# Two gate blocks computed with the first input projections, stick-breaking attention started earlier, and h written in pairs of k-tiles

## The chip, the cores and the metric

One core of a Trainium2 chip runs the whole layer. The metric is the device time of one execution in microseconds, the median of several runs. All data are float32 in memory; large matrix products are made of three products of split halves, as told below.

## What is computed

One decoder layer on 256 tokens of width 2048. The part around the change is the modulated norm, the one wide input projection and the third gate:

```python
mod = (jax.nn.silu(c) @ w_ada[l] + b_ada[l]).reshape(B, N_MOD, 1, D)
sh1, sc1, gt1, sh2, sc2, gt2 = (mod[:, j] for j in range(N_MOD))
h = rmsnorm(x, g_mix[l]) * (1.0 + sc1) + sh1
z = h @ w_in[l]
(mq, mk, mv, mo, mi, mf, dq, dk, dv, sq, sk, sv, gm, gd, gs) = split_cols(z, IN_SIZES)
...
merged = (jax.nn.sigmoid(gm) * (out_m @ w_branch[l, 0])
          + jax.nn.sigmoid(gd) * (out_d @ w_branch[l, 1])
          + jax.nn.sigmoid(gs) * (out_s @ w_branch[l, 2]))
x = x + gt1 * (merged @ w_out[l])
```

out_m, out_d and out_s are the three mixers (mLSTM, differential attention, stick-breaking attention). A gated MLP follows. w_in is 2048 x 16392, w_ada is 2048 x 12288.

## The kernel before

Every weight tile is loaded as float32 by the SP queue (`weights`, L344), rounded to a high part hi by ScalarE (L349), and its remainder lo is formed by VectorE (L351). A product is hi with both halves of the activation and lo with the high half: three matmuls for each k-tile of 128 rows and each 128 tokens (`gemm`, `mms`, L398; for blocks with features on the output partitions, L403, where the moving side is 256 tokens wide). A tick after each group of up to four k-tiles calls two queues of generators, `ada` and `side`, at the rates in `rates`: `ada` does the vector-matrix products with w_ada on VectorE (L230, L232), `side` the attention work. The order in which instructions then stand on each engine is set by a scheduler.

h needs the shift and scale, and these need w_ada: 33.6 MB for the 16 k-tiles of h. So the first projections are made in visits. `first` lists 13 column blocks (two each of sq, sk and sv of 512 columns, and seven of 440 that hold the small gates, dq, dk and dv). `visit(cis, kt1, rate)` takes the blocks `cis` on from the k-tile they had reached to k-tile kt1 (`partial`), while w_ada for the next k-tiles is loaded and multiplied in between. `make_h` (L465) writes h one k-tile at a time (ht L476 and hi L425 on ScalarE, lo L426 on VectorE), for k-tiles 0 and 1 first, 2 and 3 next (`ada_first(2)`), and then four at a time (`ada_quad`, whose VectorE products go into the tile quads). A partial sum goes to SBUF by a ScalarE copy (L556) and comes back into PSUM before the next visit by another (L545); the last visit adds it on VectorE (L558). Blocks 0 and 1 stay in PSUM (kept).

```python
visit(range(0, 9), 2, 0.62)
visit(range(9, 13), 4, 1.9)
visit(range(0, 9), 4, 1.0)
visit(range(0, 10), 8, 1.72)
visit(range(10, 13), 12, 1.36)
visit(range(0, 7), 12, 1.36)
```

After these visits h is whole. The 13 blocks are finished one after the other; when block 5 is done, stick-breaking attention (`stick`, 28 steps) joins the `side` queue. Then the first two blocks of the third gate are ordinary products over all 16 k-tiles with a sigmoid (`gates`, L860), `side` is drained, and differential attention (`diff`) joins while the other two gate blocks run. The rest (branches, mLSTM, output projection, MLP) isn't touched.

Weight loads of four k-tiles and w_ada loads share four buffers (three of rawp, and slot s3 for every fourth); loads of two k-tiles have three (tag ada). hi and lo have four buffers each, of two k-tiles.

Of the kernel before, what the change touches and what calls it, by code (L numbers as in the profile page):

```python
# [10 lines left out]
F32 = mybir.dt.float32  # L11
F32R = mybir.dt.float32r
AF = mybir.ActivationFunctionType
# [4 lines left out]
P = 128  # L18
S = 256
# [16 lines left out]
C_GM, C_GD, C_GS = 10248, 12296, 14344  # L36
# [3 lines left out]
def kernel(  # L40
# [14 lines left out]
    adap = ctx.enter_context(tc.tile_pool(name="adap", bufs=3))  # L55
# [7 lines left out]
    def slot(i, name):  # L63
        n = NT * MH * (MDH + 1) + 8 if i == 2 else 2048
        return slots.tile([P, n], F32, tag=f"s{i}", name=name)

    def bank(name):
        return mx.tile([P, 512], F32, tag="mx", name=name)

    def wide(name):  # L70
        return tmp.tile([P, 512], F32, tag="wide", name=name, bufs=3)

    def sidewide(name):
        return tmp.tile([P, 512], F32, tag="sidewide", name=name, bufs=4)

    def small(name):
        return tmp.tile([P, 256], F32, tag="small", name=name, bufs=3)

    V, A, T = nc.vector, nc.scalar, nc.tensor
# [111 lines left out]
    side = deque()  # L191
    ada = deque()
    state = {"ada": 0.0, "side": 0.0, "split": None, "load": None, "hold": None, "h": 0, "spare": None}

    def pump(queue, n):
        done = 0
        while queue and done < n:
            try:
                next(queue[0])
                done += 1  # L200
            except StopIteration:
                queue.popleft()

    def drain(queue):
        pump(queue, 1 << 30)

    rates = {"ada": 0.0, "side": 1.0}

    def tick():
        for key, queue in (("ada", ada), ("side", side)):  # L210
            state[key] += rates[key]
            n = int(state[key])
            state[key] -= n
            pump(queue, n)
# [65 lines left out]
    def ada_quad(k0, acc):  # L280

        for q in range(8):
            raw = raw_tile(2, 1024, "raw4")
            for i in range(2):
                r0, c0 = q * 256, i * D + k0 * P
                with tc.issue_after(state["load"].ins):
                    nc.sync.dma_start(raw[:, :, i * 512:(i + 1) * 512],
                                      w_ada[r0:r0 + 256, c0:c0 + 512].rearrange("(k p) f -> p k f", p=P))
            for k in range(2):
                ada_mac([acc], raw[:, k:k + 1, :], 2 * q + k, 1)  # L290
                yield
        ada_sums([acc], k0, 4)
# [39 lines left out]
    a1 = const.tile([P, KD], F32, name="a1")  # L332
    b1 = const.tile([P, KD], F32, name="b1")
# [89 lines left out]
    def split(hi, lo, src):  # L423

        A.copy(hi, src)  # L425
        return V.tensor_tensor(lo, src, hi.bitcast(F32), ALU.subtract)  # L426


    h1 = [slots.tile([P, KD // 2, 2 * S], F32R, tag=t, name="h1") for t in ("hh", "hl")]
# [3 lines left out]
    xnT_k = lambda kt: xnT[kt // 8][:, (kt % 8) * S:(kt % 8 + 1) * S]  # L433
# [29 lines left out]
            A.copy(xnT[k2 // 4][:, (k2 % 4) * 512:(k2 % 4 + 1) * 512], pb)  # L463

    def make_h(kt0, kt1):  # L465
        ts = []
        for kt in range(kt0, kt1):
            t = small("ht")
            ts.append(t)
            hi, lo = hact[0](kt), hact[1](kt)  # L470
            if kt0 == 0:
                A.activation(hi, xnT_k(kt), AF.Identity, scale=a1[:, kt:kt + 1], bias=b1[:, kt:kt + 1])
                V.tensor_scalar(t, xnT_k(kt), a1[:, kt:kt + 1], b1[:, kt:kt + 1], ALU.mult, ALU.add)
                state["split"] = V.tensor_tensor(lo, t, hi.bitcast(F32), ALU.subtract)
            else:
                A.activation(t, xnT_k(kt), AF.Identity, scale=a1[:, kt:kt + 1], bias=b1[:, kt:kt + 1])  # L476
                state["split"] = split(hi, lo, t)
        if kt0 == 0:
            state["first"] = state["split"]
        state["h"] = kt1  # L480
# [19 lines left out]
    def dest_D(i):  # L500
        def f(b):
            pieces = []
            for lo_, hi_, t in ((0, 8, None), (8, 1032, dq), (1032, 2056, dk), (2056, 3080, dv)):
                s_, e_ = max(lo_, i * 440), min(hi_, (i + 1) * 440)
                if s_ >= e_:
                    continue
                if t is None:
                    d = zif[:, b, s_:e_]
                else:
                    d = t[:, b * MW + s_ - lo_:b * MW + e_ - lo_]  # L510
                pieces.append((slice(s_ - i * 440, e_ - i * 440), d))
            return pieces
        return f

    first = []
# [5 lines left out]
        first.append(("T", C_SV + ch * 512, 512, dest_T(sv, ch), 1.0))  # L521
    for i in range(7):
        first.append(("T", C_IF + 440 * i, 440, dest_D(i), 1.0))

    def shaped(src, dst):
        return src.rearrange("p (a b) -> p a b", a=dst.shape[1]) if len(dst.shape) == 3 else src

    def partial(ci, kt0, kt1):
        orient, col0, n, dest, scale = first[ci]
        while state["h"] < kt1:  # L530
            pump(ada, 1)
        if kt0 == 0 and ci == 0:
            state["first"], done = state["mac0"], state["first"]
        pin = kt0 == 0 and ci < 2
        if kt0 == 0 and ci < 2:
            kept[ci] = [bank("kept"), bank("kept")]
        acc = kept.get(ci)


        put = acc is None and 0 < kt0 and kt1 < KD and not (kt1 == 4 and ci in (6, 8))  # L540
        if put:
            acc = [gp.tile([P, 512], F32, tag="gp", name="gp") for _ in range(2)]
            for b in range(2):
                for cs, d in dest(b):
                    A.copy(shaped(acc[b][:, cs], d), d)  # L545
        acc = gemm(orient, hact, w_in, 0, col0, n, kt0, kt1, hold=state["first"] if pin else None, hold_all=pin,
                   acc=acc)
        if kt0 == 0 and ci == 0:
            state["first"] = done
        for b in range(2):  # L550
            for cs, d in dest(b):
                if ci in kept:
                    if kt1 == KD:
                        A.activation(d, shaped(acc[b][:, cs], d), AF.Copy, scale=scale)
                elif put or kt0 == 0:
                    A.copy(d, shaped(acc[b][:, cs], d))  # L556
                else:
                    V.scalar_tensor_tensor(d, shaped(acc[b][:, cs], d), scale, d, ALU.mult, ALU.add)  # L558
        tick()

    kept = {}
# [1 line left out]
    quads = slot(4, "quads")  # L563
    ada.append(ada_first(2))
    ada.extend(ada_quad(k0, quads[:, (i % 2) * 1024:(i % 2 + 1) * 1024]) for i, k0 in enumerate((4, 8, 12)))
    done = [0] * 13

    def visit(cis, kt1, rate):
        rates["ada"] = rate
        for ci in cis:  # L570
            partial(ci, done[ci], kt1)
            done[ci] = kt1

    visit(range(0, 9), 2, 0.62)
    visit(range(9, 13), 4, 1.9)
    visit(range(0, 9), 4, 1.0)
    side.append(late_vectors())
    rates["side"] = 0.4
    visit(range(0, 10), 8, 1.72)
    visit(range(10, 13), 12, 1.36)  # L580
    visit(range(0, 7), 12, 1.36)
    drain(ada)
    drain(side)
    state["spare"] = None
# [270 lines left out]
    mg = []  # L855

    def gates(col_g, ch, dst):
        acc = gemm("T", hact, w_in, 0, col_g + ch * 512, 512, 0, KD)
        for tt in range(NT):
            A.activation(dst[tt], acc[tt], AF.Sigmoid)  # L860
        tick()

    def mg_of(ch):
        o = (ch % 2) * 512
        return [mg[ch // 2][:, tt * 1024 + o:tt * 1024 + o + 512] for tt in range(NT)]
# [31 lines left out]
        yield from ada_columns(4, bsc2_c, a2, gffn_c)  # L897

    ada.append(ada_rest())
    rates["side"] = 2.4  # L900
    for ci in range(13):
        partial(ci, done[ci], 16)
        if ci == 5:
            side.append(stick())


    rates["side"] = 2.0
    rates["ada"] = 0.9
    mg.append(slot(8, "mg0"))
    for ch in range(2):  # L910
        gates(C_GS, ch, mg_of(ch))
    drain(side)
    mg.append(slot(9, "mg1"))
    side.append(diff())
# [8 lines left out]
    for ch in range(2):  # L923
        acc = gemm("T", hact, w_in, 0, C_MO + ch * 512, 512, 0, KD)
# [6 lines left out]
    for ch in range(2):  # L931
        acc = gemm("T", hact, w_in, 0, C_MV + ch * 512, 512, 0, KD)
# [5 lines left out]
    for t, col0, f0 in ((mqT, C_MQ, 0), (mkT, C_MK, 8)):  # L938
        for ch in range(2):
            acc = gemm("H", h1act, w_in, 0, col0 + ch * 512, 512, 0, KD)  # L940
# [44 lines left out]
    for ch in range(4):  # L985
        acc = gemm("T", mact, w_out, 0, ch * 512, 512, 0, KD)
        cs = slice(ch * 512, (ch + 1) * 512)
        for tt in range(NT):
            t = wide("t512")
# [15 lines left out]
        for tt in range(NT):  # L1005
# [5 lines left out]
            with tc.issue_after(m.ins) if last else nullcontext():  # L1011
                for i in range(4):
                    k = 4 * ch + i
                    m = T.transpose(pbs[i // 2][:, (i % 2) * S + tt * P:(i % 2) * S + (tt + 1) * P],
                                    x2[tt][:, k * P:(k + 1) * P], ident)
        for i in range(4):
            k = 4 * ch + i
# [13 lines left out]
    k = 0  # L1031
    while k < KD:
# [4 lines left out]
        for j in range(m):  # L1037
            b = b2[:, k + j:k + j + 1]
            hi, lo = h2act(k + j)[:, 0:S], h2act(k + j)[:, S:2 * S]
# [9 lines left out]
    for half, (c0, c1) in enumerate(((0, 6), (6, NCH))):  # L1049
# [37 lines left out]
        for n in range(4):  # L1087
            acc = gemm("T", act, w_down, c0 * 512, n * 512, 512, 0, 4 * (c1 - c0))
            cs = slice(n * 512, (n + 1) * 512)
            for tt in range(NT):  # L1090
                t = wide("t512")
# [34 lines left out]
```

## Time and profile before

| | |
|---|---|
| median of 3 runs | 1785.43 us (1785.31 to 1785.56) |
| the profiled execution's own time | 1786.68 us |
| its span, first to last instruction | 1785.0 us |
| TensorE matmul busy | 1762.3 us (99%) |
| VectorE busy | 1302.2 us (73%) |
| ScalarE busy | 954.2 us (53%) |
| HBM traffic | 236 GB/s over the span |

The span is what the profiler saw between the first and the last instruction; the 1.7 us around it are in the execution's own time. Busy shares are averages over stages that differ, so the stretches are looked at one by one further down.

### The profile page before, as it was taken

Reading aid. Unit: us, or ns where it says so; the run is one execution under the profiler, and the core shown is the slowest. Engines: PE = TensorE matmul, PEld = TensorE weight load, DVE = VectorE, ACT = ScalarE, POOL = GpSimd, SP = SyncE. Lnnn points to the kernel's source line nnn. Section 1 sums busy time; section 2 is a strip of 40 time slices with the busy share of each in tenths; the row PEclk is TensorE's granted clock in tenths of the full one; section 3 lists DMA queues with packets and bytes.
Section 4 is the critical chain, followed back from the end, with each engine's and each line's share of the span. In section 5 each row is a group of like instructions: output and inputs, shape, how many; then the busy total and the mean of one; then the engine's idle time right before and its main releaser. Section 6 shows DMA issues by size and latency. Waiting matters only on the chain.

```text
span 1785.0 us, 23783 instructions
## 1 busy us (share of the span) xinstructions
PE 1762.3 (99%) x9168; PEld 1514.4 (85%) x9168; DVE 1302.2 (73%) x1734; ACT 954.2 (53%) x1338; POOL 16.7 (1%) x44
## 2 busy tenths in 40 slices
PE   7989999999999999999999999999999999999998
PEld 6889999888778888888888888888888888888887
DVE  6878656888878688777986577888875556666654
ACT  6667555676566566544444555555553345555432
POOL 2000000000000000000000000000000000000000
PEclk9999999999999999999999999999999999999999
DMA  9989755867767667688996557777765555555563
GB/s 330 361 315 336 281 175 166 281 223 250 252 232 260 212 219 252 230 281 285 323 307 212 185 165 247 258 258 268 267 202 201 191 189 189 189 189 189 189 214 116
DMA packets 219730, 423.33 MB, mean 237 GB/s; under 512 B 9026, under 2 KB 31674, under 8 KB 219104
## 3 DMA queue, kind: packets, MB, share of 16 engines
q1 hardware_dynamic: 217328, 417.44, 68.6%
q0 software_dynamic: 1008, 2.23, 0.4%
q10 hardware_dynamic: 1280, 2.14, 0.3%
q8 instruction: 72, 1.18, 0.3%
q14 instruction: 42, 0.34, 0.1%
HBM read 419.68 MB, written 2.10 MB: 236 GB/s over the span
## 4 chain that ended last, share of the span: by engine, by line
PE 96%; DMA 2%; DVE 1%; ACT 0%; issue 0%; SPq 0%; DVEq 0%
PE gp L398 55%; PE acch L384 32%; PE gp L403 2%; PE kept L403 2%; DMA raw<-in_w_ada_dram 1%; PE psc L688 1%; DMA raw<-in_w_in_dram 0%; PE pm L248 0%; DVE quads L232 0%; SPq L271 0%; PE pr L329 0%; DVE lo L351 0%; PE pa L713 0%; PE pm L238 0%; PE pmg L886 0%
## 5 line engine op out<-in xcount | busy, mean ns | idle before, releaser
L351 DVE TENSOR_TENSOR lo<-raw,hi 128x1024 fp32r<-128x1024 f32 (+1 forms) x608 | 724.8, 1208 | 363.0 <-ACT hi L349 325.9
L349 ACT CAST hi<-raw 128x1024 fp32r<-128x1024 f32 (+1 forms) x608 | 619.2, 1039 | 551.0 <-PE gp L398 348.7
L398 PE MATMUL gp<-hi,h 128*128 128x512 f32 (+1 forms) x1600 | 412.5, 386 | 2.1 <-ACT hi L349 1.0
L384 PE MATMUL acch<-h,hi 128*128 128x512 f32 x1664 | 403.6, 391 | 0.2 <-DVE h L1041 0.2
L384 PEld LDWEIGHTS acch<-h,hi 128*128 128x128 f32 x1664 | 303.4, 188 | 58.3 <-DVE h L1041 1.1
L398 PEld LDWEIGHTS gp<-hi,h 128*128 128x128 f32 x1600 | 295.8, 188 | 54.9 <-ACT hi L349 2.8
L398 PE MATMUL gp<-lo,h 128*128 128x512 f32 (+1 forms) x800 | 228.3, 383 | 0.0
L384 PEld LDWEIGHTS acch<-h,lo 128*128 128x128 f32 x1664 | 217.3, 191 | 10.8
L384 PE MATMUL acch<-h,lo 128*128 128x256 f32 x1664 | 220.8, 282 | 0.0
L232 DVE SCALAR_TENSOR_TENSOR acc<-araw,ccol,acc 128x512 f32<-128x512 f32 x240 | 179.0, 746 | 2.8 <-DMA araw<-in_w_ada_dram 1.1
L398 PEld LDWEIGHTS gp<-lo,h 128*128 128x128 f32 x800 | 149.7, 188 | 25.3 <-issue 0.3
L398 PE MATMUL gp<-hi,atl 128*128 128x512 f32 x352 | 137.0, 389 | 0.0
L398 PE MATMUL gp<-hi,ath 128*128 128x512 f32 x352 | 136.9, 389 | 0.0
L398 PE MATMUL gp<-lo,ath 128*128 128x512 f32 x352 | 105.8, 389 | 0.0
L398 PEld LDWEIGHTS gp<-lo,ath 128*128 128x128 f32 x352 | 66.1, 188 | 13.8
L398 PEld LDWEIGHTS gp<-hi,ath 128*128 128x128 f32 x352 | 66.1, 188 | 13.8
L398 PEld LDWEIGHTS gp<-hi,atl 128*128 128x128 f32 x352 | 66.0, 188 | 13.7
L232 DVE SCALAR_TENSOR_TENSOR quads<-raw,ccol,quads 128x1024 f32<-128x1024 f32 x45 | 57.7, 1281 | 11.1 <-DMA raw<-in_w_ada_dram 10.6
L398 PE MATMUL gp<-hi,mgl 128*128 128x512 f32 x128 | 50.3, 393 | 0.0
L398 PE MATMUL gp<-hi,mgh 128*128 128x512 f32 x128 | 50.0, 392 | 0.0
L1066 DVE SCALAR_TENSOR_TENSOR y<-gsum,cols,y 128x255 f32<-128x255 f32 (+1 forms) x88 | 41.4, 478 | 3.3 <-ACT y L1064 2.9
L403 PE MATMUL kept<-h,hi 128*128 128x256 f32 x256 | 39.1, 290 | 2.9 <-ACT h L425 1.1
(365 smaller groups left out, 1605.3 us busy)
## 6 DMA issues: line engine op xcount, KB each, us to landing
raw<-in_w_in_dram SPq DMA_DIRECT2D x98, 1024.0 KB, 5.1
raw<-in_w_up_dram SPq DMA_DIRECT2D x88, 1024.0 KB, 5.1
araw<-in_w_ada_dram SPq DMA_DIRECT2D x128, 512.0 KB, 5.9
raw<-in_w_down_dram SPq DMA_DIRECT2D x44, 1024.0 KB, 5.1
raw<-in_w_ada_dram SPq DMA_DIRECT2D x62, 512.0 KB, 7.4
raw<-in_w_branch_dram SPq DMA_DIRECT2D x24, 1024.0 KB, 6.3
raw<-in_w_in_dram SPq DMA_DIRECT2D x25, 880.0 KB, 5.6
raw<-in_w_out_dram SPq DMA_DIRECT2D x16, 1024.0 KB, 5.0
```

Of the source, the lines that this page charges most:

```text
L232: state["mac"] = V.scalar_tensor_tensor(acc, raw[:, k, :], ccol[:, kt:kt + 1], acc, ALU.mult, ALU.add)
L349: A.copy(hi[:, :, :n], raw[:, k0:k0 + 2, :n])
L351: state["split"] = V.tensor_tensor(lo[:, :, :n], raw[:, k0:k0 + 2, :n], hi[:, :, :n].bitcast(F32), ALU.subtract)
L384: T.matmul(acc[t][:, 0:m], lhsT=w[k // 2][:, k % 2, sl], rhs=ah(s0 + k)[:, 0:m], start=start, stop=s0 + k == kt1 - 1 and w is (wh if flip ...
L398: T.matmul(o, lhsT=a(s0 + k)[:, sl], rhs=wk[:, :n], **kw)
L403: T.matmul(o, lhsT=wk[:, sl], rhs=a(s0 + k), **kw)
L688: T.matmul(pcs[cc][:, o], lhsT=qT[cp, qs], rhs=kT[cp, ks], start=True, stop=True)
L1066: V.scalar_tensor_tensor(yf[:, sft:S], src[:, 0:S - sft], wc(2 - sft), yf[:, sft:S], ALU.mult, ALU.add)
```

## The change

Two column blocks of the third gate (columns C_GS to C_GS + 1024) become blocks 13 and 14 of `first`. Their partial sums lie in four tiles of 512 columns that are idle at that time: one accumulator tile of w_ada (tag acc) and three of the tag wide. Their last visit adds the sum on VectorE and applies the sigmoid from SBUF. The list of visits and its rates change. stick is appended at the same place, after block 5, but blocks 13, 6 to 12 and 14 with more k-tiles left now follow, at the side rate 2.6 instead of 2.4, and w_ada for the MLP starts at rate 0.5 there instead of after the 13 blocks. For k-tiles from 2 on, make_h rounds and splits two k-tiles with one instruction each.

```diff
     def make_h(kt0, kt1):
-        ts = []
-        for kt in range(kt0, kt1):
-            t = small("ht")
-            ts.append(t)
+        for kt in range(kt0, kt1, 1 if kt0 == 0 else 2):
             hi, lo = hact[0](kt), hact[1](kt)
...
             else:
-                A.activation(t, xnT_k(kt), AF.Identity, scale=a1[:, kt:kt + 1], bias=b1[:, kt:kt + 1])
-                state["split"] = split(hi, lo, t)
+                t = sidewide("ht")
+                for j in range(2):
+                    A.activation(t[:, j * S:(j + 1) * S], xnT_k(kt + j), AF.Identity, scale=a1[:, kt + j:kt + j + 1],
+                                 bias=b1[:, kt + j:kt + j + 1])
+                both = h1[kt // 8][:, kt % 8:kt % 8 + 2, :]
+                state["split"] = split(both[:, :, 0:S], both[:, :, S:2 * S], t.rearrange("p (k s) -> p k s", k=2))
...
+    gsp = []
+    for ch in range(2):
+        first.append(("T", C_GS + ch * 512, 512, lambda b, ch=ch: [(slice(0, 512), gsp[ch][b])], 1.0))
...
                     V.scalar_tensor_tensor(d, shaped(acc[b][:, cs], d), scale, d, ALU.mult, ALU.add)
+                    if ci > 12:
+                        A.activation(mg_of(ci - 13)[b], d, AF.Sigmoid)
...
     visit(range(0, 9), 2, 0.62)
-    visit(range(9, 13), 4, 1.9)
-    visit(range(0, 9), 4, 1.0)
+    gsp.extend([[adap.tile([P, 512], F32, tag="acc", name="gsp", bufs=2), wide("gsp")], [wide("gsp"), wide("gsp")]])
+    visit(range(9, 15), 4, 1.4)
+    visit(range(0, 9), 4, 1.15)
     side.append(late_vectors())
     rates["side"] = 0.4
-    visit(range(0, 10), 8, 1.72)
-    visit(range(10, 13), 12, 1.36)
-    visit(range(0, 7), 12, 1.36)
+    visit([13, 14, *range(0, 10)], 8, 1.55)
+    visit([*range(10, 13)], 8, 1.55)
+    visit([13, 14, *range(0, 6)], 12, 1.55)
...
-    rates["side"] = 2.4
-    for ci in range(13):
+    mg.append(slot(8, "mg0"))
+    for ci in (*range(6), 13, *range(6, 13)):
         partial(ci, done[ci], 16)
         if ci == 5:
             side.append(stick())
-
-
-    rates["side"] = 2.0
-    rates["ada"] = 0.9
-    mg.append(slot(8, "mg0"))
-    for ch in range(2):
-        gates(C_GS, ch, mg_of(ch))
+            rates["ada"], rates["side"] = 0.5, 2.6
+
+
+    rates["ada"], rates["side"] = 0.9, 2.0
+    partial(14, done[14], 16)
     drain(side)
```

Where instructions stand now, at three places. The first is VectorE at the start of the visits to k-tile 8: the remainders (lo) of w_in tiles and the products with w_ada (quads). In the kernel before:

```order
L351 TENSOR_TENSOR lo_1166<-raw_1159,hi_1165 128x1024
L232 SCALAR_TENSOR_TENSOR quads_308<-raw4_1218,ccol_124,quads_308 128x1024 x2
L232 SCALAR_TENSOR_TENSOR quads_308<-raw4_1287,ccol_124,quads_308 128x1024 x2
L351 TENSOR_TENSOR lo_1229<-raw_1226,hi_1228 128x1024
L351 TENSOR_TENSOR lo_1233<-raw_1226,hi_1232 128x1024
L351 TENSOR_TENSOR lo_1314<-raw_1311,hi_1313 128x1024
```

And in the changed kernel, where raw_1177 is the first four-k-tile load of block 13 and raw_1221 that of block 14:

```order
L426 TENSOR_TENSOR h1_138<-ht_1108,h1_138 128x2x256
L351 TENSOR_TENSOR lo_1151<-raw2_1148,hi_1150 128x2x440
L351 TENSOR_TENSOR lo_1180<-raw_1177,hi_1179 128x1024
L351 TENSOR_TENSOR lo_1184<-raw_1177,hi_1183 128x1024
L232 SCALAR_TENSOR_TENSOR quads_308<-raw4_1213,ccol_124,quads_308 128x1024
L563 SCALAR_TENSOR_TENSOR dq_304<-gp_1146,dq_304 128x152
L563 SCALAR_TENSOR_TENSOR dk_305<-gp_1146,dk_305 128x288
L563 SCALAR_TENSOR_TENSOR dq_304<-gp_1147,dq_304 128x152
L563 SCALAR_TENSOR_TENSOR dk_305<-gp_1147,dk_305 128x288
L232 SCALAR_TENSOR_TENSOR quads_308<-raw4_1213,ccol_124,quads_308 128x1024
L351 TENSOR_TENSOR lo_1224<-raw_1221,hi_1223 128x1024
```

Two loads of w_ada, four products in all, stood ahead of a w_in remainder; now one load, two products, does.

The second is ScalarE at the same place: ht and the h casts, casts of w_in tiles (hi), and the copies that bring partial sums back into PSUM (gp from dq, skT or gsp). Before:

```order
L476 ACTIVATE ht_1058<-xnT0_140,b1_135,a1_134 128x256
L556 COPY dq_304<-gp_1014 128x440
L164 COPY cols_131<-pv_1417 128x223
L545 COPY gp_1015<-dq_304 128x440
L425 CAST h1_138<-ht_1050 128x256
L425 CAST h1_138<-ht_1054 128x256
L425 CAST h1_138<-ht_1058 128x256
L349 CAST hi_1099<-raw_1097 128x1024
L349 CAST hi_1103<-raw_1097 128x1024
L476 ACTIVATE ht_1062<-xnT0_140,b1_135,a1_134 128x256
```

And in the changed kernel:

```order
L476 ACTIVATE ht_1103<-xnT0_140,b1_135,a1_134 128x256 x2
L476 ACTIVATE ht_1108<-xnT0_140,b1_135,a1_134 128x256 x2
L349 CAST hi_1124<-raw2_1122 128x2x440
L561 COPY sv_303<-gp_1040 128x512
L425 CAST h1_138<-ht_1103 128x2x256
L561 COPY sv_303<-gp_1041 128x512
L425 CAST h1_138<-ht_1108 128x2x256
L349 CAST hi_1150<-raw2_1148 128x2x440
L550 COPY gp_1118<-dq_304 128x440
L550 COPY gp_1119<-dq_304 128x440
L349 CAST hi_1179<-raw_1177 128x1024
```

All of h up to k-tile 7 is now written ahead of the casts that need it, and the copy that opens block 7's visit (gp_1118) stands behind both h casts and two w_in casts.

The third is ScalarE in stick-breaking attention, where e and z lie in the tile ez and the gate in mg. In the changed kernel:

```order
L640 ACT_TABLE_LOAD
L640 ACTIVATE ez<-ez 128x768
L349 CAST hi<-raw 128x1024 x2
L565 ACT_TABLE_LOAD
L565 ACTIVATE mg_2421<-gsp 128x512 x2
L425 CAST osh<-po 128x512
L349 CAST hi<-raw 128x1024
L614 ACTIVATE ez<-ez 128x768
L349 CAST hi<-raw 128x1024
L616 ACT_TABLE_LOAD
L616 ACTIVATE ez<-ez 128x768
L617 ACT_TABLE_LOAD
```

The sigmoid of block 13 stands between two steps of a pair of heads and adds a table load on either side of it; over the whole program ScalarE has 41 table loads instead of 38.

## Rows read from the trace of the kernel before

**Rows 1.** The page: busy time of each engine, share of the span, instructions.

```profile
PE 1762.3 (99%) x9168; PEld 1514.4 (85%) x9168; DVE 1302.2 (73%) x1734; ACT 954.2 (53%) x1338; POOL 16.7 (1%) x44
```

**Rows 2.** Stretches: us, then PE, PEld, DVE, ACT, POOL busy, PEclk, DMA share, GB/s.

```profile
46.00:60.00 14.00, 12.77 (x67) 10.77 (x66) 11.92 (x18) 9.79 (x21) 0.00 (x0) 1.00 1.05 384
60.00:126.00 66.00, 60.79 (x397) 56.65 (x396) 54.15 (x61) 40.33 (x65) 0.00 (x0) 1.00 0.92 329
106.00:112.00 6.00, 3.95 (x31) 3.54 (x30) 6.00 (x7) 5.00 (x9) 0.00 (x0) 1.00 0.61 204
120.00:126.00 6.00, 3.71 (x31) 3.51 (x30) 5.96 (x6) 2.00 (x2) 0.00 (x0) 1.00 0.86 299
200.00:1025.00 825.00, 825.00 (x4109) 697.51 (x4108) 635.72 (x902) 459.50 (x640) 4.99 (x10) 1.00 0.71 241
1050.00:1775.00 725.00, 725.00 (x3852) 626.80 (x3851) 494.68 (x622) 347.14 (x456) 1.95 (x4) 1.00 0.63 211
```

**Rows 3.** TensorE in order of time: start, length, what, and in brackets idle and releaser.

```profile
105.97 1.58 PE L403 MATMUL kept<-h,hi 128*128 128x256 f32 x12
108.63 0.50 PE L403 MATMUL kept<-h,hi 128*128 128x256 f32 x2 [1.08 <-ACT h L425]
110.10 2.05 PE L403 MATMUL kept<-h,hi 128*128 128x256 f32 x15 [0.97 <-ACT hi L349]
...
123.56 0.50 PE L403 MATMUL gp<-h,lo 128*128 128x256 f32 x2 [2.29 <-DVE lo L351]
```

**Rows 4.** VectorE and ScalarE in order of time, where h grows by k-tiles.

```profile
119.76 2.60 DVE L232 SCALAR_TENSOR_TENSOR quads<-raw,ccol,quads 128x1024 f32<-128x1024 f32 x2 [3.81 <-DMA raw<-in_w_ada_dram]
...
56.37 1.10 ACT L476 ACTIVATE ht<-xnT,b,a 128x256 f32<-128x256 f32 x2
...
108.16 0.42 ACT L425 CAST h<-ht 128x256 fp32r<-128x256 f32 x1
108.99 2.02 ACT L349 CAST hi<-raw 128x1024 fp32r<-128x1024 f32 x2
```

**Rows 5.** The chain that ended last, in order of time: start, length, what.

```profile
816.13 32.69 PE gp L398 x144
```

**Rows 6.** Stretch of the visits, and two with attention and w_ada work, columns as above.

```profile
25.00:200.00 175.00, 167.74 (x1006) 155.05 (x1006) 142.83 (x164) 114.12 (x193) 0.00 (x0) 0.99 0.95 338
275.00:300.00 25.00, 25.00 (x130) 23.43 (x129) 19.37 (x31) 15.18 (x18) 0.00 (x0) 1.00 0.49 163
850.00:875.00 25.00, 25.00 (x115) 20.67 (x115) 24.28 (x30) 11.00 (x13) 0.48 (x1) 1.00 0.92 311
```

**Rows 7.** Groups by line and shape: count, busy us, mean ns, idle before.

```profile
L351 DVE TENSOR_TENSOR lo<-raw,hi 128x880 fp32r<-128x880 f32 x56 | 59.1, 1071 | 19.5 <-ACT hi L349 14.0 <-PE gp L398 4.6 <-ACT dv L556 0.6
L232 DVE SCALAR_TENSOR_TENSOR acc<-araw,ccol,acc 128x512 f32<-128x512 f32 x240 | 179.0, 746 | 2.8 <-DMA araw<-in_w_ada_dram 1.1
L426 DVE TENSOR_TENSOR h<-ht,h 128x256 fp32r<-128x256 f32 x14 | 5.5, 419 | 2.5 <-ACT h L425 2.5
L558 DVE SCALAR_TENSOR_TENSOR sv<-gp,sv 128x512 f32<-128x512 f32 x4 | 2.7, 686 | 0.5 <-PE gp L398 0.5
L230 DVE TENSOR_SCALAR quads<-raw,ccol 128x1024 f32<-128x1024 f32 x3 | 2.2, 749 | 0.0
L349 ACT CAST hi<-raw 128x1024 fp32r<-128x1024 f32 x552 | 568.6, 1050 | 519.4 <-PE gp L398 322.8 <-issue 86.1 <-PE acch L384 61.2
L349 ACT CAST hi<-raw 128x880 fp32r<-128x880 f32 x56 | 50.6, 929 | 31.6 <-PE gp L398 25.9 <-DMA raw<-in_w_in_dram 5.2 <-ACT hi L349 0.5
L545 ACT COPY gp<-sv 128x512 f32<-128x512 f32 x12 | 7.1, 594 | 0.3
```

**Rows 8.** 260 to 400 us: stick's tiles ez and spA alone (PE, PEld, DVE, ACT), a table load.

```profile
260.00:400.00 140.00, 5.88 (x32) 5.44 (x32) 22.25 (x44) 15.16 (x20) 1.00 0.64 216
260.00:400.00 140.00, 7.16 (x12) 2.47 (x4) 1.00 0.64 216
L609 ACT ACT_TABLE_LOAD x4 | 5.1, 1283 | 0.1
```

More of the change, by code (lines that the diff above doesn't have):

```diff
@@ L465, in make_h @@
     def make_h(kt0, kt1):
-        ts = []
-        for kt in range(kt0, kt1):
-            t = small("ht")
-            ts.append(t)
+        for kt in range(kt0, kt1, 1 if kt0 == 0 else 2):
             hi, lo = hact[0](kt), hact[1](kt)
             if kt0 == 0:
+                t = small("ht")
                 A.activation(hi, xnT_k(kt), AF.Identity, scale=a1[:, kt:kt + 1], bias=b1[:, kt:kt + 1])
@@ L565 @@
     ada.extend(ada_quad(k0, quads[:, (i % 2) * 1024:(i % 2 + 1) * 1024]) for i, k0 in enumerate((4, 8, 12)))
-    done = [0] * 13
+    done = [0] * 15
     def visit(cis, kt1, rate):
```

## The prediction

> **What bounds the kernel now.** I read the page first, then the stretches, then TensorE's stops, and last the queues behind them. TensorE is busy 99% of the span [rows 1], but the stretches show where the rest lies. From 200 to 1025 us and from 1050 to 1775 us TensorE isn't idle at all [rows 2]. Work that is only moved there gives nothing, as long as nothing new stops TensorE. Between 46 and 60 us its idle time is 14 - 12.77 = 1.23 us, between 60 and 126 us 66 - 60.79 = 5.21; of that 2.05 lie at 106 to 112 us, 2.29 at 120 to 126, and 0.87 elsewhere in it [rows 2]. Start to start a stop costs some 0.15 us more than its idle time, since one 256-wide matmul follows another by 0.12 us while its tail still counts as busy: twelve began at 105.97, and the next at 108.63, 1.22 us late for 1.08 of idle [rows 3]. With five stops the loss after 60 us is 5.21 + 5 x 0.15 = 6.0 us; before, 1.23 + 4 x 0.17 = 1.9 us. The granted clock is full in all these stretches [rows 2], so none of this is the clock's.
>
> Why it stops: the largest wait (2.29 us, to 123.56) is for a lo of VectorE, and VectorE had been idle for 3.81 us before 119.76, at two products whose w_ada hadn't landed; their 2.60 us and the lo were then between the landing and TensorE [rows 3, 4]. The two stops at 107 to 110 us are for ScalarE: the fourth h cast (108.16) and the w_in casts behind it (108.99) [rows 3, 4]. So it is loads that are short, and queue order at the point where h grows by four k-tiles.
>
> **Bytes and matmuls, visit by visit.** One k-tile of a 512-wide block is 128 x 512 x 4 B = 0.262 MB and six matmuls; 144 of them took 32.69 us [rows 5], so 1.36 us. Four k-tiles of h cost 8.4 MB of w_ada. The queues delivered 338 GB/s from 25 to 200 us [rows 6]. The visits to k-tile 4 were 34 such units (4 blocks x 4, 9 x 2): 46.3 us of TensorE, and 8.9 + 8.4 = 17.3 MB, 51.2 us of loads if w_ada for the next four k-tiles is to be there: 4.9 us short. Those to k-tile 8 were 40 units, 54.5 us against 18.9 MB or 55.9 us: 1.4 short. Together 6.3 us, about the 6.0 lost. The third group (52 units, 70.8 us against 65.1) has room.
> With the change the first group has 42 units: 57.2 us against 19.4 MB or 57.4 us, 0.2 short. The second has 60: 81.7 against 71.4, 10.3 to spare. The third has only 32: 43.6 against 49.7, 6.1 short, but loads run ahead into it from the 10.3 before: by the new rates about 48 of 56 ada steps are taken when it begins. So the shortage falls from 6.3 to 0.2 us.
>
> **The change part by part.**
> - Matmuls: none added, none removed. Blocks 13 and 14 are 2 x 96 matmuls of 512 columns in either kernel, now in four visits. TensorE's own time stays: 0.
> - ScalarE: 12 copies out and 8 back for the new blocks, 20 x 0.594 [rows 7] = 11.9 us, less 8 small ones that block 6 loses with one visit. In the visits the engine is busy 114 of 175 us [rows 6], and a 512-wide block takes 4 x 0.594 + 2 x 1.050 = 4.5 us [rows 7] of the 5.45 that its 24 matmuls take. Covered, but narrowly; without cover it would be up to 11.9 us.
> - VectorE: four more final adds, 4 x 0.686 = 2.7 us [rows 7], long after the stops. Covered.
> - h in pairs: 14 subtractions of 256 become 7 of 512. VectorE saves 14 x 0.419 - 7 x 0.686 = 1.1 us [rows 7], ScalarE about as much. At k-tiles 2 and 3 the cast now stands behind two casts of the next load, and the stops before 60 us may move by half a microsecond either way. I take 0, so the 1.9 us stay.
> - Loads: the 8 loads of 1 MB for the two blocks go ahead of part of w_ada on SP's queue, into the same four buffers, each free once the load four before it is used. Counted in the sums above.
> - A new wait: block 7's opening copy (into gp_1118) now stands on ScalarE behind four ht, two h casts, two casts and two copies out, which begin when the w_ada sums leave TensorE. The sums' way over VectorE has a 0.749 product in it [rows 7], 1.2 us in all. The rest is back to back, where each takes some 0.1 us less than its mean, as two ht took 1.10 us [rows 4]: 4 x 0.50 + 2 x 0.55 + 2 x 0.85 + 2 x 0.50, and 0.6 for the copy. That is 7.6 us. TensorE has 18 matmuls of 512 and 12 of 440 columns meanwhile, 6.5 us. So it stops for 1.1 us. Queued behind that copy are block 7's other copy and block 13's casts. The bounds: 0 if the sums come early, 2.4 (what the two stops at this place cost now) if a w_in cast comes late.
> - stick: 22.25 + 7.16 = 29.4 us of VectorE on its main tiles [rows 8] over 28 steps, 1.05 a step. At 2.6 steps a tick, with two lo of 440 columns (2.1), half an ada step (0.75) [rows 7] and the adds (0.5), VectorE has 6.1 us a tick, as much as TensorE with stick's matmuls, for 11 ticks. It was at 19.37 of 25 us there; but 24.28 of 25 went without a stop at 850 us [rows 6], and four lo buffers, two ticks of lead, stand between. Cost 0; with that cover gone, what VectorE is over, a tick.
>
> The sum: 6.0 lost after 60 us, of which 0.2 stays as shortage and 1.1 comes as the new stop: 4.7 us gained. The profiled execution took 1786.68 us, which makes it 1782.0; the median shown, 1785.43, lies 1.25 lower, so I predict **1780.7 us**. Bounds of this sum: all 7.9 us gone gives 1777.5, nothing gone 1785.4.
>
> **A rule against the change.** Three table loads are added where block 13's sigmoid falls among stick's functions. One takes 1.283 us [rows 8], all three 3.85; ScalarE is busy 15.18 of 25 us there and TensorE never idle [rows 6], so I take 0. With 3.85 us on TensorE's path 0.85 of the gain would be left, 1784.6 us; that is part of the second rival. The Trainium skill, "ScalarE: Activation LUTs", section "Table sets: the hidden batching unit", advises to batch activation calls by table set, which the change breaks once.
>
> **The rivals.**
> - All stops go, those before 60 us too: 1785.4 - 7.9 = 1777.5 us. For it: the early waits are mostly for late data as well. Against: the first visit and its loads are the same. Chance 0.05.
> - Queue order, not bytes, stops TensorE. Each time h grows by four, sums, ht, casts and products come together, and stops like those at 107 to 110 us (2.4) and at 121 to 123.6 (2.4) come back; only the rest (6.0 - 4.8 = 1.2) goes. That gives 1784.2 us, no measurable change. For it: ScalarE's queue has such an order again. Against: VectorE has one w_ada load, not two, ahead of the next lo. Chance 0.22, and 0.04 for the table loads on the path.
> - Slower: VectorE can't carry stick at 2.6 steps a tick with ada beside it. It decides once VectorE's share is over 100% for longer than the two ticks of lead. With one step too much, 1.05 us a tick over 11 ticks, TensorE waits 11.6 us, less the 4.7 gained: 1792.3 us. For it: 6.1 against 6.1. Against: 2.4 steps a tick went without a stop. Chance 0.12.
>
> **How the numbers follow.** A measurement of this kernel can tell 0.2%, 3.6 us, from no change: faster is below 1781.9 us, slower above 1789.0. The forecast has 0.57; its own range, by the new stop's bounds of 0 and 2.4 us and half a microsecond for h, is 1779.1 to 1782.5. Faster takes it and the first rival, 0.62; the same 0.22 + 0.04 = 0.26; slower 0.12. The range for all, 1777.8 to 1786.0 us, takes in the second rival and leaves out the first and the third, 0.17.
>
> **What would show it.** Right: TensorE idle between 60 and 126 us falls from 5.2 to 1 or 2 us, with a wait for a ScalarE copy where block 7 is resumed; no idle from 126 us on; VectorE at 90% or more while stick runs; quads' products wait for w_ada less than 3.81 us. Wrong: stops of 2 us or more between 60 and 126 us, for a lo behind quads' products or for casts (second rival), or idle of TensorE between 260 and 400 us, for a lo or for stick's operands (third).

## The result and the profile after

The changed kernel took 1793.60 us (median of 5, 1792.85 to 1794.74), the kernel before in the same call 1785.43 (1784.39 to 1786.12). The ratio is 1.0046 with a 95% interval of 1.0034 to 1.0058: 8.2 us slower, where 4.7 us faster was forecast. The profiled execution took 1794.74 us, its span is 1793.0, against 1785.0 before. All rows below are of that execution until another is named.

The busy times from the page, to be set against [rows 1], show TensorE busy 5 us longer, though it has the same 9168 instructions:

```profile
PE 1767.3 (99%) x9168; PEld 1517.0 (85%) x9168; DVE 1303.3 (73%) x1731; ACT 964.2 (54%) x1346; POOL 16.9 (1%) x44
```

The stretches, with the columns of [rows 2], show where the time lies:

```profile
46.00:60.00 14.00, 12.09 (x66) 10.41 (x64) 11.08 (x16) 9.53 (x19) 0.00 (x0) 1.00 1.04 371
60.00:126.00 66.00, 64.80 (x355) 57.62 (x356) 56.15 (x62) 46.37 (x72) 2.65 (x5) 1.00 0.97 345
126.00:200.00 74.00, 73.09 (x441) 67.96 (x440) 57.86 (x57) 53.29 (x94) 0.00 (x0) 1.00 0.94 330
260.00:400.00 140.00, 139.81 (x717) 125.39 (x715) 112.31 (x166) 81.68 (x93) 0.00 (x0) 1.00 0.68 230
399.00:404.00 5.00, 1.07 (x6) 0.64 (x5) 2.89 (x2) 4.59 (x5) 0.00 (x0) 0.85 0.73 275
404.00:409.00 5.00, 5.00 (x12) 3.86 (x13) 1.58 (x3) 3.32 (x4) 0.00 (x0) 0.50 0.00 0
563.00:570.00 7.00, 4.53 (x28) 3.27 (x27) 6.49 (x14) 2.53 (x7) 0.12 (x1) 1.00 0.66 226
570.00:1025.00 455.00, 455.00 (x2168) 379.76 (x2167) 347.56 (x470) 230.42 (x303) 3.12 (x6) 1.00 0.72 246
```

The forecast gain is there: idle time between 60 and 126 us fell from 5.21 to 1.20 us. What was not forecast stands at 399 us (3.93 us idle, then a stretch at half the granted clock, in which a busy TensorE does half the work) and at 563 us (2.47 us idle), where the kernel before had none [rows 2]. TensorE's rows at these places, in order of time (start, length, what, and in brackets idle time and what ended it):

```profile
54.66 0.47 PE L398 MATMUL gp<-hi,h 128*128 128x440 f32 x1 [0.71 <-ACT hi L349]
...
110.70 1.07 PE L398 MATMUL gp<-hi,h 128*128 128x440 f32 x4 [1.20 <-ACT gp L550]
...
177.14 1.87 PE L398 MATMUL gp<-hi,h 128*128 128x440 f32 x8 [0.91 <-ACT gp L550]
...
399.10 0.71 PE L398 MATMUL gp<-lo,h 128*128 128x512 f32 x2
403.73 2.08 PE L398 MATMUL gp<-hi,h 128*128 128x512 f32 x4 [3.93 <-ACT mg L868]
...
410.09 0.62 PE L398 MATMUL gp<-lo,h 128*128 128x512 f32 x2
...
564.71 0.63 PE L238 MATMUL pm<-ident,acc 128*128 128x128 f32 x4 [0.40 <-DVE acc L232]
565.84 0.63 PE L756 MATMUL ptf<-ident,od 128*128 128x128 f32 x4 [0.51 <-DVE od L744]
566.89 1.53 PE L756 MATMUL ptf<-ident,od 128*128 128x128 f32 x12 [0.42 <-DVE od L744]
569.57 1.20 PE L398 MATMUL gp<-hi,h 128*128 128x512 f32 x4 [1.15 <-ACT mv L940]
```

Start to start, the first new stop costs 4.1 us. From 403.73 to 410.09, 16 matmuls of 512 columns took 6.36 us where 16 x 0.227 [rows 5] are 3.63: 2.7 us for the half clock. The second stop costs 3.1 in four pieces. Together 9.9. The early stops cost 5.0 us (2.5 before 60 us, 1.4 at 110, 1.1 at 177) where they cost 7.9 before: 2.9 gained. A second gain has no term in the prediction's sum: TensorE's first matmuls on h begin sooner. In the kernel before:

```profile
27.83 1.22 PE L403 MATMUL kept<-h,hi 128*128 128x256 f32 x4 [0.82 <-ACT h L472]
```

and in the changed kernel:

```profile
26.56 0.84 PE L403 MATMUL kept<-h,hi 128*128 128x256 f32 x4 [0.41 <-ACT h L470]
```

At the first matmul on 440 columns (46.16 us before, 45.14 now) 1.0 us of this is left. So 9.9 - 2.9 - 1.0 = 6.0 of the 8.0 us between the spans are accounted for. The other 2.0 are not idle time: they lie in the 5.0 us that TensorE counts as busy longer, of which the half clock is 2.7 and the tails at two more stops some 0.3. Where they arise isn't shown.

**Why it stops.** ScalarE around the first stop, in the changed kernel:

```profile
399.38 0.58 ACT L425 CAST osh<-po 128x512 fp32r<-128x512 f32 x1 [3.93 <-PE po L651]
399.86 1.91 ACT L662 ACTIVATE dsq<-dq 128x2048 f32<-128x2048 f32 x1
401.79 1.28 ACT L868 ACT_TABLE_LOAD   x1
403.08 1.09 ACT L868 ACTIVATE mg<-gp 128x512 f32<-128x512 f32 x2
```

and the same instructions in the kernel before:

```profile
385.99 0.59 ACT L425 CAST osh<-po 128x512 fp32r<-128x512 f32 x1 [2.48 <-PE po L643]
386.48 1.92 ACT L654 ACTIVATE dsq<-dq 128x2048 f32<-128x2048 f32 x1
...
397.11 1.28 ACT L860 ACT_TABLE_LOAD   x1
398.40 0.60 ACT L860 ACTIVATE mg<-gp 128x512 f32<-128x512 f32 x1
```

The third gate has four blocks of 512 columns; the sigmoids at L868 (L860 before) read the sums of its third block out of PSUM. In the changed kernel these sums were whole when the fourth block began, near 393 us; but the sigmoids stand on ScalarE behind the cast of stick's last output, which itself waits for matmuls (po) that TensorE has among those of the fourth block, and behind diff's first square. The pool for these sums has three banks (L59), a block takes two: the fourth block could run eight k-tiles of its first 128 tokens in the free bank, and then needed the second. Before, stick's end fell into the middle of the third block, ten us ahead of its sigmoids. At 564 us TensorE waits for diff's output od: its transposes must be done before the copies of mv (the value projection of mLSTM) may write, since od and mv share a tile. The first of the four pieces, 0.40 us, waits for a product with w_ada that stands ahead of od's scaling on VectorE.

Why stick ends late: ScalarE's instructions on stick's tile ez, one group by line (count; minimum, median and maximum in ns; first and last start). Before, its four pairs of heads began from 279.0 to 363.3 us:

```profile
L606 ACT ACTIVATE ez<-ez x4: 837/844/848, 279.0 to 363.3; 128x768 f32<-128x768 f32 x4
```

and in the changed kernel from 289.4 to 374.9:

```profile
L614 ACT ACTIVATE ez<-ez x4: 842/844/847, 289.4 to 374.9; 128x768 f32<-128x768 f32 x4
```

A pair takes (363.3 - 279.0) / 3 = 28.1 us before and 28.5 now. Its start is 10.4 us later, not sooner, although the title has it started earlier: "after block 5" is the same place in the program, but that place comes later. The last sums of blocks 4 and 5 (sv) are added on VectorE until 270.6 us before,

```profile
L558 DVE SCALAR_TENSOR_TENSOR sv<-gp,sv x4: 683/684/691, 262.0 to 270.6; 128x512 f32<-128x512 f32 x4
```

and until 280.2 in the changed kernel:

```profile
L563 DVE SCALAR_TENSOR_TENSOR sv<-gp,sv x4: 683/685/687, 271.6 to 280.2; 128x512 f32<-128x512 f32 x4
```

The visits of blocks 13 and 14 put 24 units of 1.36 us ahead of it, and blocks 6 and 10 to 12 moved 16 narrower ones behind it (440 columns, six matmuls of 0.20 us each: 1.2): 32.6 - 19.2 = 13.4 us more, less the 3.9 gained by then, makes 9.5, and 9.6 were measured. So stick ends 13.4 us later (399.38 against 385.99), while the gate blocks around it come earlier (the fourth begins at 392.88, against 398.10).

### The profile page after: what moved, and what is told of

It is laid out like the page before. It is cut to its first block, busy times and chain, and to the rows that moved or that the text cites. A ratio compares the mean times of both kernels' runs of the same rounds, so it can differ in the third digit from the quotient of the medians.

```text
span 1793.0 us, 23772 instructions
## 1 busy us (share of the span) xinstructions
PE 1767.3 (99%) x9168; PEld 1517.0 (85%) x9168; DVE 1303.3 (73%) x1731; ACT 964.2 (54%) x1346; POOL 16.9 (1%) x44
## 4 chain that ended last, share of the span: by engine, by line
PE 96%; ACT 1%; DMA 1%; DVE 1%; issue 0%; SPq 0%; DVEq 0%; ACTq 0%
PE gp L398 54%; PE acch L384 32%; PE kept L403 3%; PE gp L403 3%; PE psc L696 1%; DMA raw<-in_w_ada_dram 1%; DMA raw<-in_w_in_dram 0%; ACT hi L349 0%; PE pm L248 0%; ACT ht L476 0%; DVE lo L351 0%; PE pr L329 0%; PE pa L721 0%; PE pmg L894 0%; PE pdt L681 0%
## 5 line engine op out<-in xcount | busy, mean ns | idle before, releaser
L398 PEld LDWEIGHTS gp<-lo,h 128*128 128x128 f32 x800 | 150.2, 188 | 26.2 <-issue 1.0
```

The lines of the kernel that those rows point to most:

```text
L398: T.matmul(o, lhsT=a(s0 + k)[:, sl], rhs=wk[:, :n], **kw)
```

## The experiments

The theory (called the position theory below): both new stops come from where stick and diff end against the gate and mv blocks, and this is set by when stick starts and by its own 28 us a pair of heads. The rivals: VectorE can't carry stick at the new rates (the prediction's third rival); or the pairs of k-tiles of h are the cause. "Before" in the brackets is the kernel before, timed in the same call, then the ratio to it with its 95% interval.

**h one k-tile at a time again** (make_h as in the kernel before, the rest as changed).

> The changed kernel with h written one k-tile at a time again. Position theory (the two new stops, 4.1 and 3.1 us, come from stick and diff ending about 13 us later): nothing about them changes, 1793.6 us within 1.5, the idle time of 4 us near 400 us stays, as does a stretch of half clock behind it; the stops before 60 us move by at most 1 us. If the pairs of h were the cause, this run would lie at 1789 us or below.

1793.06 us (before 1786.18; ratio 1.0040, 1.0026 to 1.0053). The stop near 400 us is the same (4.1 us start to start). The stops at 110 and 177 us are gone, and one near 61 us became 1.6 us; early stops then cost 2.9 us, not 5.0. So pairs do put the copies that reopen a block behind more ScalarE work, but the medians differ by 0.5 us only, which these runs can't tell from nothing. The traces show what pairs give in return: TensorE's first matmuls on h begin at 26.53 to 26.76 us in the nine traces with pairs and at 27.65 to 27.97 in the seven with single k-tiles (27.97 here). By what path is open. Pairs are not the cause of the loss.

**The rates of before.**

```diff
-            rates["ada"], rates["side"] = 0.5, 2.6
+            rates["ada"], rates["side"] = 0.0, 2.4
```

> The changed kernel with the rates of before while stick runs (side 2.4, no w_ada products). VectorE rival (VectorE can't carry stick at 2.6 steps with half a w_ada step beside it): the stop near 400 us goes, 1785 to 1788 us. Position theory (a pair of heads takes 28 us whatever the rate, by the length of its own chain): the pairs still start some 28 us apart, the stop stays, 1792 to 1795 us.

1793.87 us (before 1786.18; 1.0040, 1.0027 to 1.0052): the VectorE rival, which wanted 1785 to 1788, falls by the time. Stick's pairs begin here:

```profile
L614 ACT ACTIVATE ez<-ez x4: 843/846/847, 289.3 to 367.9; 128x768 f32<-128x768 f32 x4
```

They came closer, 26.2 us apart, with fewer steps a tick but without the products with w_ada. So VectorE's load has some share in the pace; which of the two rates did it, this run can't say. The first stop shrank to 1.62 us of idle time (some 1.8 us in all, where it had cost 4.1 and 2.7), and no half clock followed; the second grew, and one did:

```profile
401.53 1.21 PE L398 MATMUL gp<-hi,h 128*128 128x512 f32 x4 [1.62 <-ACT mg L868]
...
561.30 0.63 PE L756 MATMUL ptf<-ident,od 128*128 128x128 f32 x4 [1.17 <-DVE od L744]
```

I had expected the first stop unchanged. That was a miss: the two stops traded time, and the sum was the same.

**Stick sooner: blocks 13 and 14 without their third visit** (and more w_ada steps a tick in that visit, since it has fewer ticks).

```diff
-    visit([13, 14, *range(0, 6)], 12, 1.55)
+    visit(range(0, 6), 12, 2.1)
```

> The changed kernel without the third visit of blocks 13 and 14 (they go from k-tile 8 to 16 behind stick's start), 8 units of 1.36 us, so stick starts 10.9 us sooner. Position theory: stick ends near 388 us, diff starts there, both new stops (7.1 us with the half clock, and 3.1) go: 1783.4 us, up to 2 us more if the loads of the visits now come late. VectorE rival: the same work lies in the same stretch, so the stop stays: 1791 us or more.

1787.96 us (before 1786.18; 1.0008, 1.0000 to 1.0017): 5.6 us less than the changed kernel, and 4.6 above what the position theory gave. The first stop is gone, though the order on ScalarE is the same (cast, square, table load, sigmoid): all of it comes 8.5 us earlier, while TensorE still has work in the free bank.

```profile
390.91 0.59 ACT L425 CAST osh<-po 128x512 fp32r<-128x512 f32 x1 [2.70 <-PE po L651]
391.40 1.92 ACT L662 ACTIVATE dsq<-dq 128x2048 f32<-128x2048 f32 x1
393.33 1.28 ACT L868 ACT_TABLE_LOAD   x1
394.63 0.60 ACT L868 ACTIVATE mg<-gp 128x512 f32<-128x512 f32 x1
```

The second stop stayed, against the expectation; its last piece, and the granted clock after it (third last column of the stretch):

```profile
561.74 1.30 PE L398 MATMUL gp<-hi,h 128*128 128x512 f32 x4 [2.18 <-ACT mv L940]
```

```profile
562.00:566.00 4.00, 4.00 (x12) 3.08 (x12) 2.10 (x3) 2.32 (x5) 0.00 (x0) 0.58 0.02 4
```

Here diff ends as early as in the kernel before (its first transposes at 556.90 against 556.95), but the gate, branch and mo blocks (mo is mLSTM's output gate) are done sooner. So the two stops are separate: the early gain itself brings TensorE to a diff that isn't whole.

**The reverse: the kernel before with stick two blocks later.**

```diff
-        if ci == 5:
+        if ci == 7:
             side.append(stick())
```

> The kernel before with stick joined two blocks later (after block 7, not 5), some 10 us. Position theory: a stop of TensorE for a sigmoid of the third gate near 398 us appears, and one where diff must be whole near 560 us: 1785.4 + 3 to 10 = 1788 to 1796 us. If only the amount of work in the changed kernel's stretch counted (VectorE rival), nothing would change: 1785.4 us within 1.

1792.91 us (before 1786.18; 1.0037, 1.0025 to 1.0050). Stick's pairs begin at 291.4 us, 12.4 later. With nothing else changed the first stop appears, with the same releaser; a half clock follows, and near 566 us there is a small second stop (0.68 us of idle time):

```profile
407.38 2.08 PE L398 MATMUL gp<-hi,h 128*128 128x512 f32 x4 [4.39 <-ACT mg L860]
```

This is the strongest support for the position theory: a later start of stick alone costs 6.7 us in a kernel that has nothing else of the change.

**mv later.** To take the second stop away I put the two mv blocks, with the drain of diff ahead of them, behind the four mq and mk blocks: in the changed kernel, in the one with stick sooner, in the kernel before as a control, and with single k-tiles of h.

```diff
-    drain(side)
-    mv = slots.tile([P, NT, MH, MDH + 1], F32, tag="s2", name="mv")
...
+    drain(side)
+    mv = slots.tile([P, NT, MH, MDH + 1], F32, tag="s2", name="mv")
...
     side.append(mlstm(mqT, mkT, sig))
```

> The changed kernel with the two mv blocks (value projection of mLSTM), and the drain ahead of them, behind the four mq and mk blocks, so that diff has some 90 us more before it must be whole. Position theory: the second stop (3.1 us near 564 us) goes, the first (7.1 us with the half clock) stays: 1790.5 us. Rival (the whole loss hangs on the first stop, and what diff does later is hidden): 1793.6 us.

> Both together: blocks 13 and 14 without their third visit (stick 12 us sooner) and mv last. Position theory: neither stop, 1788.0 less the 4.0 us of stop near 556 us and some half clock behind it: 1783 to 1784 us. Rival (a stop of this kind comes back at the next place that needs stick or diff): 1787 us or more.

> The kernel before with mv last, a control: it has no stop where diff must be whole, so moving mv gives nothing: 1785.4 to 1786.2 us, the kernel before, within 1. If it is faster by over 1 us, what mv last gives isn't the stop.

> As the second, and h one k-tile at a time again. In the run with single k-tiles alone the stops near 109 and 176 us (1.4 and 1.1 us, each for a copy back into PSUM behind the pair's casts) were not there, one of 1.6 us near 61 us was: 5.0 us of early stops against 2.9. If pairs cost that, 2 us below the second run: 1781 to 1782 us; if it was chance of the order, the same as the second.

All four missed their times: 1802.68 (before 1786.90; ratio 1.0088, 1.0074 to 1.0101), 1791.97 (1.0032, 1.0020 to 1.0043), 1795.19 (1.0052, 1.0039 to 1.0064) and 1791.20 (1.0029, 1.0018 to 1.0040). The control, the kernel before with mv last, shows why; its TensorE:

```profile
542.85 3.87 PE L748 MATMUL ptf<-ident,od 128*128 128x128 f32 x16 [6.70 <-DVE od L736]
```

A mq block takes two of its four sums from the four banks (`mx`, L60) that diff uses, and the other two from the pool of three (the expectation of the run with od in another tile, below, says all four; by the kernel it is two). That fits what the trace shows: with mq next, diff's transposes stand on TensorE ahead of a mq block's matmuls, some 14 us before they did (542.85 against 556.95), and TensorE waits 6.70 us for od to be scaled. The edit moved the place where diff must be whole to an earlier time, not to a later one. The rival of the second run, that a stop comes back at the next place that needs diff, held, and so did the fourth's "the same as the second" (1791.20 and 1791.97).

**od in another tile.** diff's od takes the tile that dk leaves, and mv no longer waits for it; the drain moves two blocks on, just ahead of mq.

```diff
-        od = slot(2, "od")[:, 0:2048]
+        od = slot(6, "od")
...
-        oh = slots.tile([P, KM, S], F32R, tag="s6", name="odh")
-        ol = slots.tile([P, KM, S], F32R, tag="s7", name="odl")
+        oh = slots.tile([P, KM, S], F32R, tag="s7", name="odh")
+        ol = slots.tile([P, KM, S], F32R, tag="s0", name="odl")
...
-        num = slot(0, "num")
+        num = slot(6, "num")
...
-    drain(side)
     mv = slots.tile([P, NT, MH, MDH + 1], F32, tag="s2", name="mv")
...
+    drain(side)
     mqT, mkT = slot(3, "mqT"), slot(4, "mkT")
```

> The changed kernel with od (diff's output) in the tile that dk leaves, so that the mv blocks no longer wait for diff; diff must be whole two blocks later. Position theory: the second stop (3.1 us near 564 us) goes, no new one comes as long as diff's transposes stand before the mq blocks (which take all four banks of the pool that diff uses), the first stop stays: 1793.6 - 3.1 = 1790.5 us. Rival (a wait of the same size comes where diff must be whole now): 1793 us or more.

1790.41 us (before 1786.62; 1.0025, 1.0016 to 1.0033), as the position theory had it. After the first stop, which is unchanged, TensorE isn't idle again up to 1040 us:

```profile
402.60 1.65 PE L398 MATMUL gp<-hi,h 128*128 128x512 f32 x3 [3.93 <-ACT mg L868]
```

**The same, and diff joined one gate block later.**

```diff
     mg.append(slot(9, "mg1"))
+    gates(C_GS, 2, mg_of(2))
     side.append(diff())
     rates["side"] = 2.9
-    for ch in range(2, 4):
-        gates(C_GS, ch, mg_of(ch))
+    gates(C_GS, 3, mg_of(3))
```

> The same, and diff joined one gate block later, so that diff's first square (1.9 us) stands behind the sigmoids of gate block 2 on ScalarE, no longer ahead. Position theory: the first stop is then the cast of stick's last output (to 399.9 us), the table load (1.28) and a sigmoid (0.6): 2.2 us in place of 4.1, and without the stretch of half clock (3.0) if the clock stays full: 1790.5 - 4.9 = 1785.6 us. Rival (the square isn't what holds the sigmoid; stick's cast alone does): 1789 us or more.

1785.95 us (before 1786.62; 1.0000, 0.9992 to 1.0009), 4.5 below the run before it. ScalarE now has the sigmoids ahead of the square, and TensorE's stop is 2.12 us:

```profile
399.58 0.59 ACT L425 CAST osh<-po 128x512 fp32r<-128x512 f32 x1 [3.92 <-PE po L651]
400.19 1.28 ACT L868 ACT_TABLE_LOAD   x1
401.48 1.08 ACT L868 ACTIVATE mg<-gp 128x512 f32<-128x512 f32 x2
402.45 1.91 ACT L662 ACTIVATE dsq<-dq 128x2048 f32<-128x2048 f32 x1
```

```profile
402.13 2.07 PE L398 MATMUL gp<-hi,h 128*128 128x512 f32 x4 [2.12 <-ACT mg L868]
```

So one ScalarE instruction of 1.91 us, wrong in its place, was that much of the stop; the rest of the 4.5 us fits the half clock that followed a shorter time or not at all. Some half clock stayed in the profiled execution (four matmuls from 402.13 to 404.00, 1.87 us where 4 x 0.227 are 0.91), which took 1788.06, 2.1 above the median. The granted clock on record, a mean over each execution, is 1.000 in the five that took 1785.1 to 1785.4 us and 0.998 in the four at 1788, so the spread goes with the clock; where in an execution without a profile it fell wasn't seen.

**Both remedies: stick sooner and od in dk's tile**, first with h in pairs, then with single k-tiles.

> Blocks 13 and 14 without their third visit (stick 12 us sooner), and od in dk's tile. Position theory: neither stop, 1788.0 - 4.0 (stop near 556 us) - 1.6 (eight matmuls' worth of half clock behind it) = 1782.4 us, 3.8 below the kernel before in the same call. Rival (the next place takes the stop): 1786 us or more.

> As the one before, with h one k-tile at a time again: the stops of 1.4 and 1.1 us near 109 and 176 us go, one of 1.6 us near 61 us comes in place of 0.6: 1 to 2 us below it, 1780.5 to 1781.5 us. If pairs cost nothing, the same.

1782.30 us (before 1786.62; ratio 0.9979, 0.9970 to 0.9988) and 1782.26 (0.9977, 0.9968 to 0.9986): faster than both kernels. The stretches of the first of them show the early gain kept and the rest without a stop:

```profile
60.00:126.00 66.00, 64.81 (x356) 57.48 (x355) 55.95 (x63) 47.05 (x74) 1.81 (x4) 1.00 0.97 347
126.00:200.00 74.00, 73.09 (x450) 68.33 (x449) 57.86 (x56) 53.31 (x93) 0.00 (x0) 1.00 0.93 326
200.00:650.00 450.00, 450.00 (x2417) 389.94 (x2417) 353.34 (x527) 266.19 (x388) 2.39 (x4) 1.00 0.67 230
```

The pairs of h again made no difference in the median.

**Two controls:** the changed kernel with `rates["side"]` at 5.2 while stick runs, and the kernel before with od in dk's tile.

> The changed kernel with side steps at 5.2 a tick, not 2.6, while stick runs. If the chain of a pair sets the pace (the next pair needs the tile ez free), pairs still start 26 to 30 us apart, stick ends near 399 us, both stops stay: 1793.6 us within 2. If the rate sets it, pairs come about 14 us apart, stick ends near 345 us and both stops go: 1783 to 1784 us, or VectorE falls behind and TensorE stops for lo between 290 and 345 us.

> The kernel before with od in dk's tile alone, a control. It has no stop where diff must be whole, so the edit gives nothing: the kernel before within 1 us. If it is 2 us or more faster, the gain of the two runs that beat both kernels is not the early stops'.

1793.64 us (before 1785.99; 1.0044, 1.0031 to 1.0057) and 1786.00 (1.0003, 0.9993 to 1.0012). With the doubled rate the scheduler wrote the same order of instructions on TensorE, VectorE and ScalarE as at 2.6, so the run measures the changed kernel once more; what it shows is that the rate no longer decides anything there, not what does. The pairs begin 28.5 us apart, from 288.3 to 373.8.

And od's tile gives nothing by itself, so the 4.3 us of the best runs (2.1 to 5.4 by the interval) belong to the new visits.

## Why the prediction was wrong

Point by point, in the prediction's order:

- **What bounds the kernel, and the bytes.** Held, as far as waits can show it. Idle time between 60 and 126 us went from 5.21 to 1.20 us (forecast: 1 to 2). VectorE's waits for w_ada at the quads' products became fewer and shorter. From 60 to 200 us (us in total, times, longest) they were, before:

```profile
DVE quads L232 <- DMA raw<-in_w_ada_dram: 10.6, 5, 3.8
```

and in the changed kernel, where the longest, at 188.84 us, was followed by no stop of TensorE:

```profile
DVE quads L232 <- DMA raw<-in_w_ada_dram: 2.4, 2, 1.9
```

The sum itself counts the blocks of 440 columns as if they had 512. With 440/512 of the bytes and 1.2 us a unit, the shortage falls from 8.2 to 1.4 us, not from 6.3 to 0.2, so that 6.3 came so close to the 6.0 us lost was partly luck.

- **The new stop at block 7's opening copy.** It came where it was forecast, for a ScalarE copy behind the h casts: 1.1 us forecast, 1.20 idle and 1.4 start to start measured. The same order comes once more where h grows to k-tile 12 (0.91 us at 177 us); I had priced one of the two, so the forecast "no idle from 126 us on" failed there already.
- **h in pairs, before 60 us.** Forecast 0 within half a microsecond; 1.9 became 2.5, about as allowed. That TensorE's first matmuls on h begin 1.3 us sooner was not foreseen.
- **The sum of the early stops** was thus 2.9 us gained, not 4.7, or 3.9 with the earlier start; the best runs, which keep this gain and little else, gained 4.3 (2.1 to 5.4). The mechanism was right, the size uncertain by about as much as a measurement can tell.
- **stick: the step that failed.** It read: "1.05 a step. At 2.6 steps a tick ... VectorE has 6.1 us a tick ... Cost 0". It took the rate for stick's pace and VectorE's load for the only limit. By the rate, 28 steps would be done in 11 ticks, 60 us; from ScalarE's first instruction on ez to the last cast they took 107 us before and 110 in the changed kernel. The pace is 28 us a pair, 4 us a step, in both kernels, at 2.4, 2.6 and 5.2 steps a tick; over all traces it is 26.2 (w_ada's products gone) to 30.0 (the kernel before with stick late). The trace of before had it in plain sight: the instructions of ez at L606 begin 28 us apart, and I read only their busy time [rows 8]. With the pace given, the start decides, and the start moved back by 10.4 us; that block 5's end comes later follows from my own count of units, which I used for bytes and not for stick. From there two deadlines were missed: the sigmoids' place behind stick's cast and diff's square (4.1 us, and 2.7 of half clock), and diff's end (3.1 us). The second was missed for two reasons, a later stick and earlier work around it, as the run with stick sooner shows. And VectorE, for which the forecast wanted 90% or more, was busy 92.64 of the 110 us from 289 to 399 us, in which stick runs: 84%.
- **The table loads.** Held at 0: the loads ahead of the two blocks' sigmoids (L565, 279.6 and 367.6 us) stand in stretches without a stop. The load inside the first new stop (401.79) is not an added one; the kernel before has it at 397.11.
- **The third rival** gave 1792.3 us, 1.3 from what was measured, by another mechanism: VectorE at more than it can carry between 260 and 400 us. It was busy 112.31 of 140 us there, TensorE wasn't idle until the stop at the end of that stretch, and the run with the old rates was as slow. So a number nearly right came from a wrong cause. The second rival's kind of wait, ScalarE's queue order, is what happened, but at the sigmoids of the third gate and not where h grows.

Still open: what within a pair sets the 28 us. That the four pairs share the tile ez, so that the next can't begin before the last matmuls of this one, fits, but no run gave stick a second tile; the 26.2 us without w_ada's products suggest that what else VectorE has to do has a part in it.

## What to carry to other kernels

A part that runs beside the main work has a pace of its own: read in the trace how far apart its rounds start, not only how busy they are, before a change is credited with making it sooner or denser. Then ask for its end, not its share: list what must wait for it and what stands behind its last instruction on each engine. And when the main work gets faster, the side work's deadlines come sooner by as much, so a gain of a few microseconds can be lost at a wait that had just enough room before.

## What the runs showed of the hardware

The price of a stop was more than its length. In the changed kernel TensorE stood idle for 3.93 us, and in the stretch right after, from 404 to 409 us, the granted clock was 0.50, 1.2 GHz, which cost 2.7 us on top; the same came after 4.39 us idle in the kernel before with stick late. The length of the idle time alone doesn't decide it: after 2.12 us (diff joined later) ten matmuls took 3.98 us, 402.13 to 406.11, where 10 x 0.227 are 2.27, so seven or eight ran at the half clock; after the 2.29 us at 123.56 us of the kernel before the clock stayed full [rows 2, 3]. The granted clock (third last column) with stick late, and with diff joined later:

```profile
405.00:410.00 5.00, 2.62 (x6) 2.13 (x7) 2.29 (x1) 3.29 (x5) 0.00 (x0) 0.50 0.00 0
```

```profile
400.00:405.00 5.00, 2.88 (x8) 2.29 (x8) 1.29 (x2) 4.97 (x6) 0.00 (x0) 0.72 0.58 218
```

I had priced no stop with a clock behind it. The Trainium skill, "TensorE: Matmul & The Clock Gate", section "Why this matters for your kernels", says that idle gaps of TensorE between bursts of matmuls, once they are long enough, are followed by a drop in its throughput. The rows of 3.93 and 4.39 us agree; those of 2.12 and 2.29, where the shorter gap was followed by the half clock and the longer was not, don't go by length.

A table load between two ScalarE instructions cost what it shows and no more: the square ended at 401.77 us, the load ran from 401.79 for 1.28, the sigmoid began at 403.08.
